# Half-batch tiles with two 24 KB runs of each of 64 lines, and one ring of three buffers for all tiles

## The chip, the cores and the metric

The kernel runs on one core of a Trainium2 chip. The metric is the device time of one execution in microseconds (us). Times of a kernel are given as the median of several executions; profiles show one execution in detail. The profile names the engines DVE (VectorE), ACT (ScalarE), POOL (GpSimd), SP (SyncE) and PE (TensorE, unused here); sixteen DMA engines move data between HBM and the on-chip memory of 128 partitions.

## The reference

The input x is float32 of shape (16, 64, 64, 64): batch b, channel c, height h, width w, 16.78 MB. The output holds all windows of 8 by 8 at a stride of 4, so 15 by 15 window positions (i, j):

```python
n_h = (h - window_size) // stride + 1
n_w = (w - window_size) // stride + 1
for i in range(n_h):
    for j in range(n_w):
        h_start = i * stride
        w_start = j * stride
        result[:, i, j] = x[:, :, h_start:h_start + window_size, w_start:w_start + window_size].copy()
```

The result has the shape (16, 15, 15, 64, 8, 8), 58.98 MB. Nothing is calculated; each input value is copied to up to four places. One window position of one image is 64 x 8 x 8 floats, 16 KB. For a fixed (b, i) the fifteen windows j lie one behind the other in memory; such a "line" is 15 x 16 KB = 240 KB, and there are 16 x 15 = 240 lines.

## The kernel before, in words

**The input on chip.** The tile L holds the whole input: partition p = 64 ch + 4 b + hq has the channels of half ch (32 of them) and the rows 16 hq to 16 hq + 15 of image b, in 4 KB per channel. The batch is also split in two halves y of 8 images (QP = 32 partitions for each ch and y). The loads are on three queues. ACT and SP first load the first FC = (8, 7) channels of each half into a staging area S, 64 partitions wide, which lies in the same memory as the output buffers (GG); DVE and ACT then copy it to its places in L (the loop over `moves`). SP and POOL load the other channels directly into L, for y = 0 first and then for y = 1 (the function `load`). All this comes before any output work in each engine's order.

**The output tiles.** A tile is a buffer in GG in which each partition holds one piece of one line, to be written as one row. DVE and ACT fill it by copies from L (with `stream_shuffle` on DVE where rows must move to the next partition or as another form of copy), and POOL writes it to HBM with an indirect DMA (`scatter`): an index per partition says which row of the output it is. The output is seen in two ways: `o_v` has rows of one window (CFREE = 4096 floats, 16 KB), `o_l` has rows, called runs here, of one and a half windows (LF = 6144 floats, 24 KB), NR = 10 to a line. Run k of a line begins with window 3k/2; `line(k)` lists its pieces: two half-windows of one channel half ch (places 0 and 2 of the row, from windows j and j + 1) and one half-window of the other (place 1). `windows(f, c, r, j, m)` is the view of L with m neighbouring windows, which overlap by half.

Four kinds of tiles are made:

- `part(y, j)`: a half-batch tile. Its 128 partitions hold the windows j and j + 1 of each of 64 lines (8 images, 4 hq, the line offsets s = 0 and 1 within a row block), as 16 KB rows. It needs only the half y of the input. Eight copies of 32 partitions x 2048 floats fill it, three on ACT and five on DVE. Its index is `idx_y`.
- `plain(k)`: run k of 128 lines (all 16 images, line offsets 0 and 1), 24 KB rows. Two copies on ACT, one copy and one shuffle on DVE. Its index is `idx`.
- `cross(k)`: run k of the lines with offsets 2 and 3; those with offset 3 take their lower half from the next row block, so a shuffle moves data by one partition. 112 of 128 rows are written. Its indices are `idx_lo` and `idx_hi` in turns.
- The last run of the lines with offsets 0 and 1 (loop at the end), written by two plain DMAs from SP, each of 64 rows.

**The order.** Three tiles part(0, 0), part(0, 2), part(0, 4) come first, as they need only the first half of the batch; then plain(4), part(1, 0), plain(5), part(1, 2), plain(6), part(1, 4); then plain(7), cross(0) to cross(4), plain(8), cross(5) to cross(9); then the last run. The half-batch tiles write windows 0 to 5, that is runs 0 to 3, of their lines.

**The buffers.** GG is 3 x 24 KB per partition. `tile_()` hands out the buffers: the first three tiles (EARLY) get three 16 KB places at its beginning, the fourth gets the third 24 KB buffer, and from there the tiles take the three 24 KB buffers in turn. A fill waits until the store that last read its memory has landed. The stores are declared free of each other, since each writes rows of its own. A DMA on POOL's queue also waits for the landing of the DMA eight before it, whose semaphore it uses.

**Queues.** POOL issues 16 loads and then the 21 scatters in the order of the tiles; they share one DMA queue (q0). SP issues its staging loads, 14 direct loads, and the two last stores (q1). ACT issues four staging loads (q10).

Of the kernel before, what the change touches and what calls it, by code (L numbers as in the profile page):

```python
# [10 lines left out]
def kernel(  # L11
# [8 lines left out]
    P = nc.NUM_PARTITIONS  # L20

    B, C, H, W = x.shape
    Bo, NH, NW, Co, WSo, WSo2 = out.shape
    WS = int(window_size)
    ST = int(stride)
# [4 lines left out]
    ALU = mybir.AluOpType  # L30
    CH = 2
# [4 lines left out]
    NWIN = NH * NW  # L36
    CFREE = C * WS * WS
    HP = P // CH
    YB = 8
    NY = B // YB  # L40
    QP = YB * HQ
# [10 lines left out]
    L = Lt[:, :, 0 : RB * W].rearrange("p c (r w) -> p c r w", r=RB)  # L52
# [12 lines left out]
    def itile(name):  # L65
        return ipool.tile([P, 1], i32, name=name)

    pi, tb, tq, tc_, te, tu, idx, idx_y, idx_lo, idx_hi = (
        itile(n) for n in ("pi", "tb", "tq", "tc", "te", "tu", "idx", "idx_y", "idx_lo", "idx_hi")
    )  # L70


    LF = 3 * CFREE // 2
    NR = NW * CFREE // LF
# [4 lines left out]
    def bits(d, shift, mask):  # L79
        nc.vector.tensor_scalar(out=d[:, :], in0=pi[:, :], scalar1=shift, scalar2=mask, op0=ALU.logical_shift_right, op1=ALU.bitwise_and)  # L80

    def mul(d, a, m):
        nc.vector.tensor_scalar(out=d[:, :], in0=a[:, :], scalar1=float(m), scalar2=None, op0=ALU.mult)

    def tt(d, a, b, op):
        nc.vector.tensor_tensor(out=d[:, :], in0=a[:, :], in1=b[:, :], op=op)  # L86
# [4 lines left out]
    def far(d, a, value):  # L91
        nc.vector.tensor_scalar(out=d[:, :], in0=a[:, :], scalar1=float(value), scalar2=FAR, op0=ALU.is_equal, op1=ALU.mult)
# [7 lines left out]
    tt(tu, tb, tc_, ALU.add)  # L100
    mul(idx, tu, NR)
    bits(tq, 5, 1)
    mul(tq, tq, 1 - YB * NWIN)
    mul(tu, tu, NW)
    tt(idx_y, tu, tq, ALU.add)
    far(tb, te, HP + HQ - 1)
    tt(idx_hi, idx, tb, ALU.add)
    far(te, te, HQ - 1)
# [5 lines left out]
    NG = 3  # L114
# [5 lines left out]
    GG = gpool.tile([P, NG * LF], f32)  # L120
# [3 lines left out]
    for q in range(HQ):  # L124
        for ch in range(CH):
            s = S[ch][QP + q : QP + q + (B - 1) * HQ + 1 : HQ]
# [14 lines left out]
    for n, (y, ch, c) in enumerate(moves):  # L141
        e = min(c + PC, FC[ch])
        f = slice(QP + y * QP, QP + (y + 1) * QP)
        d = slice(ch * HP + y * QP, ch * HP + (y + 1) * QP)
        copy = nc.vector.tensor_copy if n % 3 else nc.scalar.copy
        tc.keep_in_program_order(copy(out=L[d, c:e, :, :], in_=S[ch][f, c:e]))  # L146

    o_v = out.rearrange("b i j c r w -> (b i j) (c r w)")
    o_l = out.rearrange("b i j c r w -> (b i j c r w)").rearrange("(n f) -> n f", f=LF)
    nxt = [min(p + 1, 31) for p in range(32)]  # L150
    same = list(range(32))
    act, dve = nc.scalar.copy, nc.vector.tensor_copy

    def shf(out, in_, mask=same):
        nc.vector.stream_shuffle(out=out, in_=in_, mask=mask)  # L155

    def free(st):
        tc.declare_no_dep(st.ins, group="stores", reason="each store writes rows of its own")
        tc.add_to_no_dep_group("stores", st.ins)

    def scatter(g, ix, rows, first):
        f = rows.shape[1]
        st = nc.gpsimd.indirect_dma_start(  # L163
            out=rows,
            out_offset=bass.IndirectOffsetOnAxis(ap=ix[:, 0:1], axis=0),
            in_=g,
            in_offset=None,
            element_offset=first * f,
            bounds_check=rows.shape[0] - 1,
            oob_is_err=False,  # L170
        )
        free(st)

    EARLY = 3
    at = 0

    def tile_():
        nonlocal at
        at += 1
        if at <= EARLY:  # L180
            return GG[:, (at - 1) * CFREE : at * CFREE]
        n = (at - EARLY - 2) % NG
        return GG[:, n * LF : (n + 1) * LF]

    def halves(g, n):
        return g[:, 0 : n * CFREE // 2].rearrange("p (n c r w) -> p n c r w", n=n, c=CL, r=WS)

    def part(y, j):
        t = tile_()[:, 0:CFREE]
        g = halves(t, CH)  # L190
        order = [(d, ch) for ch in range(CH) for d in range(P // QP)]
        for n, (d, ch) in enumerate(order):
            s, dj = d // NY, d % NY
            cols = slice((j + dj) * ST, (j + dj) * ST + WS)
            f = (ch * NY + y) * QP
            tc.keep_in_program_order(
                (act if n % 3 == 0 else dve)(  # L197
                    out=g[d * QP : (d + 1) * QP, ch],
                    in_=L[f : f + QP, :, s * ST : s * ST + WS, cols],
                )  # L200
            )
        scatter(t, idx_y, o_v, j + y * YB * NWIN)

    def line(k):
        j, ch = 3 * k // CH, 3 * k % CH
        return (j, ch, slice(0, 3, 2), 2), (j + ch, 1 - ch, slice(1, 2), 1)

    def windows(f, c, r, j, m):  # L210
        v = L[f, c, r, j * ST : j * ST + WS]
        return bass.AP(tensor=v.tensor, offset=v.offset, ap=[v.ap[0], [ST, m], *v.ap[1:]])

    every = slice(0, CL)
    crossed = 0

    def plain(k):
        t = tile_()
        g = halves(t, 3)
        for half in range(CH):  # L220
            for j, ch, n, m in line(k):
                f = slice(ch * HP, (ch + 1) * HP)
                d = slice(half * HP, (half + 1) * HP)
                copy = (shf if m == 1 else act) if half == 0 else (dve if m == 2 else act)
                copy(out=g[d, n], in_=windows(f, every, slice(half * ST, half * ST + WS), j, m))  # L225
        scatter(t, idx, o_l, k)

    def cross(k):
        nonlocal crossed
        t = tile_()  # L230
        g = halves(t, 3)
        turn = 1 - crossed % 2
        crossed += 1
        lo, hi = slice(turn * HP, (turn + 1) * HP), slice((1 - turn) * HP, (2 - turn) * HP)
        s = NSLOT - 2
        for j, ch, n, m in line(k):
            f = slice(ch * HP, (ch + 1) * HP)
            act(out=g[lo, n], in_=windows(f, every, slice(s * ST, s * ST + WS), j, m))  # L238
            shf(out=g[hi, n, :, ST:WS], in_=windows(f, every, slice(0, ST), j, m), mask=nxt)
        for j, ch, n, m in line(k):  # L240
            f = slice(ch * HP, (ch + 1) * HP)
            dve(out=g[hi, n, :, 0:ST], in_=windows(f, every, slice((s + 1) * ST, RB), j, m))  # L242
        scatter(t, (idx_hi, idx_lo)[turn], o_l, s * NR + k)

    for n in range(EARLY):
        part(0, 2 * n)
    ready = 2 * EARLY * CFREE // LF
    for n in range(EARLY):
        plain(ready + n)
        part(1, 2 * n)  # L250
    rest = list(range(ready + EARLY, NR - 1))
    per = NR // len(rest)
    for n, k in enumerate(rest):
        plain(k)
        for m in range(n * per, (n + 1) * per):
            cross(m)


    ACT_C = 12
# [1 line left out]
    for s in range(2):  # L261
        t = tile_()
        g = halves(t, 3)
        for j, ch, n, m in line(NR - 1):
            for y in range(NY):
                d = slice(QP + y * QP, QP + (y + 1) * QP)
                f = slice(ch * HP + y * QP, ch * HP + (y + 1) * QP)
# [38 lines left out]
```

## Time and profile before

| | |
|---|---|
| Median of 3 runs | 184.75 us (184.5 to 184.81) |
| The profiled execution | 184.68 us, of which the span is 182.9 us |
| DVE busy | 138.7 us (76% of the span) |
| ACT busy | 137.5 us (75%) |
| POOL busy | 40.4 us (22%) |
| DMA | 75.80 MB in 9507 packets, mean 414 GB/s |
| HBM read, and written by the instructions' own account | 16.78 MB and 62.91 MB |

How to read it: "busy" is the time in which an engine executes instructions; issuing a DMA from SP or ACT does not count, but POOL's DMA instructions do, as POOL writes their descriptors. The span is cut into 40 slices, and each digit of a row is the busy share in tenths. "DMA" there is the mean over the sixteen DMA engines. Queue rows (q0, q1, q10) give packets, MB and the share of the sixteen engines' span. In the view of windows, a row gives for one stretch of time each engine's busy time with its number of instructions, the granted clock, the DMA share and the rate; packets are counted there from their start, so a share can be a little above 1. In the timeline and in the chain of waits a row begins with the start and the duration in us; in square brackets stands the idle time of the engine just before, and what ended it. In the rows of groups, after the count come the busy time, the mean ns of one, and the idle time before with what ended it. A row with "DMA out_dram<-GG,idx" as what ended a wait means that the engine waited for a store to land.

The bytes written by the instructions' own account count 16 rows for each crossing tile that are out of bounds and not written.

### The profile page before, as it was taken

The page shows a single profiled execution, that of the slowest core. Times are in us where ns is not written, and L with a number is a line of the kernel's source. Part 1 is how long each engine was busy: PE and PEld are TensorE (multiplying, and loading weights), DVE is VectorE, ACT ScalarE, POOL GpSimd, SP SyncE. Part 2 cuts the span into 40 slices and gives each one's busy share as a digit, 9 for nine tenths or more (in the row PEclk, how much of TensorE's full clock was granted, in tenths as well). Part 3 has the DMA queues.
Part 4 walks back from the last instruction along what each step waited for, and adds up shares of the span by engine and source line. Part 5 has one row for each costly group of instructions (what it writes and reads, how often), then busy time and mean ns, then how long its engine had stood idle before and what let it go on. Part 6 is the DMA issues. An engine that isn't in the chain of part 4 may idle for free.

```text
span 182.9 us, 453 instructions
## 1 busy us (share of the span) xinstructions
DVE 138.7 (76%) x141; ACT 137.5 (75%) x63; POOL 40.4 (22%) x42
## 2 busy tenths in 40 slices
DVE  3003997999998849979799888979769698894900
ACT  0003998999996869979899788969969697894900
POOL 7500754034340220231112202210220220240000
DMA  4999999999999999999999999999999999999995
GB/s 147 405 414 410 409 411 411 409 414 432 432 430 450 441 403 432 430 446 434 428 455 430 430 426 430 430 430 435 430 430 430 430 430 414 430 430 419 430 435 215
DMA packets 9507, 75.80 MB, mean 414 GB/s; under 512 B 2752, under 2 KB 2752, under 8 KB 6848
## 3 DMA queue, kind: packets, MB, share of 16 engines
q0 software_dynamic: 6736, 62.92, 81.3%
q1 hardware_dynamic: 2192, 10.75, 14.3%
q10 hardware_dynamic: 576, 2.10, 3.1%
q14 instruction: 3, 0.02, 0.0%
HBM read 16.78 MB, written 62.91 MB: 436 GB/s over the span
## 4 chain that ended last, share of the span: by engine, by line
DMA 75%; DVE 13%; POOL 3%; issue 2%; DVEq 1%; POOLq 0%; PEldq 0%
DMA out_dram<-GG,idx 28%; DMA out_dram<-GG,idx_lo 21%; DMA Lt<-in_x_dram 20%; DMA out_dram<-GG,idx_hi 6%; DVE GG L155 6%; POOL Lt L61 3%; DVE GG L242 2%; DVE GG L197 2%; DVE GG L269 2%; DVE GG L225 1%; DVEq L301 1%; POOL pi L77 0%; DVEq L155 0%; POOLq L163 0%; DVEq L269 0%
## 5 line engine op out<-in xcount | busy, mean ns | idle before, releaser
L238 ACT COPY GG<-Lt 64x4096 f32<-64x4096 f32 (+1 forms) x20 | 55.0, 2750 | 8.6 <-DMA out_dram<-GG,idx_lo 4.6
L155 DVE STREAM_SHUFFLE GG<-Lt 64x2048 f32<-64x2048 f32 (+1 forms) x25 | 49.2, 1969 | 0.6
L197 DVE COPY GG<-Lt 32x2048 f32<-32x2048 f32 x30 | 36.6, 1218 | 5.2 <-DMA out_dram<-GG,idx 3.6
L197 ACT COPY GG<-Lt 32x2048 f32<-32x2048 f32 x18 | 34.1, 1897 | 4.0 <-DMA out_dram<-GG,idx 2.8
L225 ACT COPY GG<-Lt 64x4096 f32<-64x4096 f32 (+1 forms) x10 | 27.5, 2750 | 3.8 <-DMA out_dram<-GG,idx_y 2.1
L146 DVE COPY Lt<-GG 32x2048 f32<-32x2048 f32 (+1 forms) x10 | 11.4, 1184 | 14.1 <-DMA GG<-in_x_dram 14.0
L242 DVE COPY GG<-Lt 64x2048 f32<-64x2048 f32 (+1 forms) x20 | 19.1, 955 | 0.5
L61 POOL DMA_DIRECT2D Lt<-in_x_dram x16 | 13.8, 871 | 15.9 <-DMA Lt<-in_x_dram 15.4
L163 POOL DMA_INDIRECT out_dram<-GG,idx_y x6 | 8.8, 1474 | 31.8 <-DVE GG L197 31.8
L146 ACT ACT_TABLE_LOAD x1 | 1.3, 1283 | 16.8 <-DMA GG<-in_x_dram 16.8
L163 POOL DMA_INDIRECT out_dram<-GG,idx_hi x5 | 6.2, 1248 | 28.7 <-DVE GG L242 17.9
L225 DVE COPY GG<-Lt 64x4096 f32<-64x4096 f32 x5 | 11.4, 2289 | 0.2
L269 ACT COPY GG<-Lt 32x1536 f32<-32x1536 f32 (+1 forms) x8 | 9.2, 1150 | 2.7 <-DMA out_dram<-GG,idx_lo 2.4
L269 DVE COPY GG<-Lt 32x2560 f32<-32x2560 f32 (+1 forms) x8 | 9.2, 1152 | 2.5 <-DMA out_dram<-GG,idx_lo 2.3
L163 POOL DMA_INDIRECT out_dram<-GG,idx x5 | 6.4, 1283 | 20.5 <-ACT GG L225 18.2
L163 POOL DMA_INDIRECT out_dram<-GG,idx_lo x5 | 4.8, 965 | 26.8 <-DVE GG L242 26.8
L146 ACT COPY Lt<-GG 32x2048 f32<-32x2048 f32 (+1 forms) x6 | 10.3, 1751 | 0.1
L155 DVE LOAD_MASK_SELECT GG<-Lt x25 | 0.2, 8 | 10.5 <-DMA out_dram<-GG,idx_lo 5.2
L80 DVE TENSOR_SCALAR tb<-pi 128x1 int32<-128x1 int32 x1 | 0.2, 154 | 1.0 <-POOL pi L77 1.0
L77 POOL IOTA pi<- 128x1 int32 x1 | 0.1, 124 | 0.4 <-PEq L301 0.4
L86 DVE CUSTOM_DVE_ANT_0 te<-te,tc 128x2 uint16<-128x2 uint16 x1 | 0.2, 160 | 0.0
L86 DVE CUSTOM_DVE_ANT_0 tb<-tb,tq 128x2 uint16<-128x2 uint16 x1 | 0.2, 159 | 0.0
(19 smaller groups left out, 2.6 us busy)
## 6 DMA issues: line engine op xcount, KB each, us to landing
Lt<-in_x_dram POOLq DMA_DIRECT2D x8, 800.0 KB, 16.1
out_dram<-GG SPq DMA_DIRECT2D x2, 1536.0 KB
Lt<-in_x_dram SPq DMA_DIRECT2D x6, 384.0 KB
GG<-in_x_dram ACTq DMA_DIRECT2D x4, 512.0 KB
Lt<-in_x_dram SPq DMA_DIRECT2D x6, 320.0 KB
GG<-in_x_dram SPq DMA_DIRECT2D x4, 448.0 KB
Lt<-in_x_dram SPq DMA_DIRECT2D x2, 704.0 KB
Lt<-in_x_dram POOLq DMA_DIRECT2D x8, 64.0 KB, 15.8
```

Of the source, the lines that this page charges most:

```text
L61: eng.dma_start(out=L[p0 : p0 + QP - HQ + 1 : HQ, c0:c1, :, :], in_=x_v[ch, y, q, :, c0:c1, :])
L80: nc.vector.tensor_scalar(out=d[:, :], in0=pi[:, :], scalar1=shift, scalar2=mask, op0=ALU.logical_shift_right, op1=ALU.bitwise_and)
L86: nc.vector.tensor_tensor(out=d[:, :], in0=a[:, :], in1=b[:, :], op=op)
L146: tc.keep_in_program_order(copy(out=L[d, c:e, :, :], in_=S[ch][f, c:e]))
L155: nc.vector.stream_shuffle(out=out, in_=in_, mask=mask)
L163: st = nc.gpsimd.indirect_dma_start(out=rows, out_offset=bass.IndirectOffsetOnAxis(ap=ix[:, 0:1], axis=0), in_=g, in_offset=None, element_ ...
L197: (act if n % 3 == 0 else dve)(out=g[d * QP : (d + 1) * QP, ch], in_=L[f : f + QP, :, s * ST : s * ST + WS, cols],)
L225: copy(out=g[d, n], in_=windows(f, every, slice(half * ST, half * ST + WS), j, m))
L238: act(out=g[lo, n], in_=windows(f, every, slice(s * ST, s * ST + WS), j, m))
L242: dve(out=g[hi, n, :, 0:ST], in_=windows(f, every, slice((s + 1) * ST, RB), j, m))
L269: copy(out=g[d, n, c0:c1], in_=windows(f, slice(c0, c1), slice(s * ST, s * ST + WS), j, m))
L301: with _tile.TileContext(nc) as tc:
```

## The change

`part(y, k)` now makes a tile with 24 KB rows: the runs k and k + 1 of each of the 64 lines of the half batch. Its pieces come from `line(k)` and `line(k + 1)`, so for each group of 32 partitions there is one copy of two windows (32 x 4096 floats) and one of one window (32 x 2048). The eight copies go by an order in which the pieces of channel half 0 come first; three of them go to ACT. The wide copies use the `windows` view, as plain tiles do.

Four such tiles, (0, 0), (0, 2), (1, 0) and (1, 2), replace the six of before; they write the runs 0 to 3 as before. The index `idx_y` is now made from `idx` with an offset in runs, one instruction less, and the view `o_v` is gone.

The order of the tiles is written out: part(0, 0), part(0, 2), plain(4), plain(5), part(1, 0), plain(6), part(1, 2), plain(7), cross(0) to cross(4), plain(8), cross(5) to cross(9), and the last run as before.

`tile_()` hands out the three 24 KB buffers in turn from the first tile on.

```diff
     bits(tq, 5, 1)
-    mul(tq, tq, 1 - YB * NWIN)
-    mul(tu, tu, NW)
-    tt(idx_y, tu, tq, ALU.add)
+    mul(tq, tq, 1 - YB * NH * NR)
+    tt(idx_y, idx, tq, ALU.add)
...
-    o_v = out.rearrange("b i j c r w -> (b i j) (c r w)")
...
-    EARLY = 3
     at = 0
 
     def tile_():
         nonlocal at
         at += 1
-        if at <= EARLY:
-            return GG[:, (at - 1) * CFREE : at * CFREE]
-        n = (at - EARLY - 2) % NG
+        n = (at - 1) % NG
         return GG[:, n * LF : (n + 1) * LF]
...
-    def part(y, j):
-        t = tile_()[:, 0:CFREE]
-        g = halves(t, CH)
-        order = [(d, ch) for ch in range(CH) for d in range(P // QP)]
-        for n, (d, ch) in enumerate(order):
-            s, dj = d // NY, d % NY
-            cols = slice((j + dj) * ST, (j + dj) * ST + WS)
-            f = (ch * NY + y) * QP
-            tc.keep_in_program_order(
-                (act if n % 3 == 0 else dve)(
-                    out=g[d * QP : (d + 1) * QP, ch],
-                    in_=L[f : f + QP, :, s * ST : s * ST + WS, cols],
-                )
-            )
-        scatter(t, idx_y, o_v, j + y * YB * NWIN)
...
+    def part(y, k):
+        t = tile_()
+        g = halves(t, 3)
+        order = [(d, *e) for c in range(CH) for d in range(P // QP) for e in line(k + d % NY) if e[1] == c]
+        for i, (d, j, ch, n, m) in enumerate(order):
+            s = d // NY
+            f = (ch * NY + y) * QP
+            tc.keep_in_program_order(
+                (act if i in (0, 6, 4 if k else 5) else dve)(
+                    out=g[d * QP : (d + 1) * QP, n],
+                    in_=windows(slice(f, f + QP), every, slice(s * ST, s * ST + WS), j, m),
+                )
+            )
+        scatter(t, idx_y, o_l, k + y * YB * NH * NR)
...
-    for n in range(EARLY):
-        part(0, 2 * n)
-    ready = 2 * EARLY * CFREE // LF
-    for n in range(EARLY):
-        plain(ready + n)
-        part(1, 2 * n)
-    rest = list(range(ready + EARLY, NR - 1))
-    per = NR // len(rest)
-    for n, k in enumerate(rest):
-        plain(k)
-        for m in range(n * per, (n + 1) * per):
-            cross(m)
+    for k in (0, 2):
+        part(0, k)
+    plain(4)
+    plain(5)
+    part(1, 0)
+    plain(6)
+    part(1, 2)
+    plain(7)
+    for k in range(NR // 2):
+        cross(k)
+    plain(8)
+    for k in range(NR // 2, NR):
+        cross(k)
```

## The prediction

> **What bounds the kernel now.** I read the page first: the span, the slices, the queues and the chain.
>
> ```profile
> span 182.9 us, 453 instructions
> DVE 138.7 (76%) x141; ACT 137.5 (75%) x63; POOL 40.4 (22%) x42
> DMA  4999999999999999999999999999999999999995
> GB/s 147 405 414 410 409 411 411 409 414 432 432 430 450 441 403 432 430 446 434 428 455 430 430 426 430 430 430 435 430 430 430 430 430 414 430 430 419 430 435 215
> DMA packets 9507, 75.80 MB, mean 414 GB/s; under 512 B 2752, under 2 KB 2752, under 8 KB 6848
> q0 software_dynamic: 6736, 62.92, 81.3%
> q1 hardware_dynamic: 2192, 10.75, 14.3%
> q10 hardware_dynamic: 576, 2.10, 3.1%
> DMA 75%; DVE 13%; POOL 3%; issue 2%; DVEq 1%; POOLq 0%; PEldq 0%
> ```
>
> The three queues together fill 81.3 + 14.3 + 3.1 = 98.7% of the sixteen DMA engines' span, and in every slice but the first and the last they are at nine tenths or more. The chain's 13% of DVE are no gap in the transfers: while that chain passes through DVE, stores issued earlier are still moving. The next view, the windows, shows it stage by stage.
>
> ```profile
> core 0: us, DVE busy (x) ACT busy (x) POOL busy (x), PEclk, DMA share, GB/s
> 3.00:43.00 40.00, 24.86 (x22) 25.22 (x15) 14.59 (x16) 1.00 1.03 408
> 45.00:91.00 46.00, 39.98 (x30) 40.56 (x18) 9.77 (x7) 1.00 1.00 431
> 91.00:175.00 84.00, 70.21 (x71) 69.71 (x30) 12.98 (x12) 1.00 1.01 432
> ```
>
> DMA share is 1.00 or more in the loads (3 to 43), in the stage that the change rewrites (45 to 91) and in the stage behind it. The rate with 16 KB rows among the stores (431 GB/s) and with 24 KB rows alone (432) is the same to 0.3%. So the span is bytes divided by rate, and an edit counts only if it changes the bytes, the rate, or makes the queue run dry.
>
> **The change part by part.** The bytes stay: six tiles of 128 rows of 16 KB are 12.6 MB, four of 128 rows of 24 KB too, and the other tiles keep their rows (lines 4 to 8, then the crossing ones, then the last). What one store occupies is read from the landings that released fills:
>
> ```profile
> 59.88 5.53 ACT L225 COPY GG<-Lt 64x4096 f32<-64x4096 f32 x2 [2.08 <-DMA out_dram<-GG,idx_y]
> 67.12 6.18 DVE L197 COPY GG<-Lt 32x2048 f32<-32x2048 f32 x5 [2.43 <-DMA out_dram<-GG,idx]
> 79.22 6.20 DVE L197 COPY GG<-Lt 32x2048 f32<-32x2048 f32 x5 [1.12 <-DMA out_dram<-GG,idx]
> 91.31 11.07 ACT L238 COPY GG<-Lt 64x4096 f32<-64x4096 f32 x4 [0.49 <-DMA out_dram<-GG,idx]
> ```
>
> The third store (16 KB rows) has landed at 59.88, the fourth (24 KB rows) at 67.12: 7.24 us. From there a store of each kind lands at 79.22 and another pair at 91.31, 12.1 us a pair, so 16 KB rows take 4.86. Six of those are 29.2 us, four of 7.24 are 29.0: minus 0.2. By the windows' rates the difference is nothing. I take minus 0.1, with minus 0.2 and 0 as its ends.
>
> The Trainium skill, page "DMA: Bandwidth & Descriptors", section "Anatomy of one DMA", gives such a store about 2.0 us of fixed time plus its bytes over 436 GB/s. Taken as a price for every store, two stores fewer would save 4 us; the landings 7.24 us apart leave no room for it, since 3.15 MB at the window's 432 GB/s are 7.28 us.
>
> The index edit drops one DVE instruction of 0.15 us:
>
> ```profile
> L83 DVE TENSOR_SCALAR tu<-tu 128x1 int32<-128x1 int32 x1 | 0.1, 148 | 0.0
> ```
>
> Its result feeds stores that wait for loads and fills long behind it, so it is worth nothing. Two store issues fewer on POOL, an engine busy for 22%, stand ahead of no work that could start sooner: nothing.
>
> What can cost something is whether each store is filled before the one ahead has left the queue. The fills are now longer, and the buffers are three of 24 KB from the start, where the first four stores had places of their own. Prices of copies:
>
> ```profile
> L197 DVE COPY GG<-Lt 32x2048 f32<-32x2048 f32 x30 | 36.6, 1218 | 5.2 <-DMA out_dram<-GG,idx 3.6 <-DMA Lt<-in_x_dram 1.0
> L155 DVE STREAM_SHUFFLE GG<-Lt 64x2048 f32<-64x2048 f32 x15 | 36.4, 2428 | 0.3
> L238 ACT COPY GG<-Lt 64x2048 f32<-64x2048 f32 x10 | 19.0, 1897 | 0.2
> L197 ACT COPY GG<-Lt 32x2048 f32<-32x2048 f32 x18 | 34.1, 1897 | 4.0 <-DMA out_dram<-GG,idx 2.8 <-DMA Lt<-in_x_dram 0.8
> L225 ACT COPY GG<-Lt 64x4096 f32<-64x4096 f32 x5 | 18.0, 3604 | 3.7 <-DMA out_dram<-GG,idx_y 2.1 <-DMA out_dram<-GG,idx_lo 1.5
> L225 DVE COPY GG<-Lt 64x4096 f32<-64x4096 f32 x5 | 11.4, 2289 | 0.2
> ```
>
> A half-batch tile becomes four copies of two windows (32x4096, a form not in this trace) and four of one. The nearest row for the two-window copy is the 64x4096 one, 2.29 on DVE and 3.60 on ACT; above it stand two 32x2048 copies, 2.44 and 3.79. I take the former: only the number of partitions differs, and ACT's 2048-element copy takes 1.897 us on 32 as on 64. With 0.02 between copies, a tile of run 0 gives DVE two wide and three narrow ones (8.3 us) and ACT two wide and one narrow (9.1); a tile of run 2 gives DVE three wide and two narrow (9.4), ACT one wide and two narrow (7.4). A plain tile stays at 5.5 us of ACT.
>
> Now the walk. In these rows the fills begin at 29.2, after the same loads, and the last load lands at 44.98:
>
> ```profile
> 29.23 5.74 ACT L197 COPY GG<-Lt 32x2048 f32<-32x2048 f32 x3 [0.76 <-DMA Lt<-in_x_dram]
> 29.64 15.35 DMA Lt<-in_x_dram
> 36.33 1.74 POOL L163 DMA_INDIRECT out_dram<-GG,idx_y  x1 [5.63 <-DVE GG L197]
> 48.62 2.39 POOL L163 DMA_INDIRECT out_dram<-GG,idx_y  x1 [4.36 <-DVE GG L197]
> ```
>
> The first store was issued at 36.33 and lay in the queue behind loads: three stores before 59.88 are 14.6 us, so the first began at 45.3 by its landing, just after the last load. The new first store is full at 29.2 + 9.1 = 38.4 and begins at the same 45.3, with seven microseconds of cover. From there the new landings are 7.24 apart: 52.5, 59.8, 67.0, 74.3, 81.5, 88.7, 96.0. The fills: the second tile ends when DVE has done both, 29.25 + 8.3 + 9.4 = 47.0. Plain 4 waits for nothing (its loads are there when ACT gets to it at 45.8) and ends at 51.8. Plain 5 needs the first store's buffer: 52.5 + 5.5 = 58.1. Half-batch tile (1, 0) needs the second's: 59.8 + 9.1 = 68.9. Plain 6 follows on ACT: 74.4. Tile (1, 2) needs the fourth's: 74.3 + 9.4 = 83.7. Plain 7 follows on DVE: 83.7 + 4.75 = 88.5. The first crossing tile needs the sixth's, 88.7, and takes 6.5, as from 91.31 to the issue at 97.83: 95.2.
>
> ```profile
> 97.83 0.97 POOL L163 DMA_INDIRECT out_dram<-GG,idx_lo  x1 [5.78 <-DVE GG L242]
> 103.44 5.52 ACT L238 COPY GG<-Lt 64x4096 f32<-64x4096 f32 x2 [1.05 <-DMA out_dram<-GG,idx]
> ```
>
> The spare time, from full until the store ahead lands, is thus 5.5 for the second store, then 8.0, 8.9, 5.4, 7.1, 5.0, 7.5 and 8.1. How much is needed is shown by the stores of before with the least:
>
> ```profile
> 74.08 0.96 POOL L163 DMA_INDIRECT out_dram<-GG,idx_y  x1 [7.43 <-DVE GG L197]
> 78.88 1.69 POOL L163 DMA_INDIRECT out_dram<-GG,idx  x1 [3.84 <-ACT GG L225]
> 86.19 0.96 POOL L163 DMA_INDIRECT out_dram<-GG,idx_y  x1 [5.63 <-DVE GG L197]
> 91.10 0.96 POOL L163 DMA_INDIRECT out_dram<-GG,idx  x1 [3.95 <-ACT GG L225]
> ```
>
> They were issued 5.1 (to 79.22), 5.2 (to 79.22 + 4.86), 5.1 (to 91.31) and 5.1 us (to 91.31 + 4.86) before the landing ahead, and the 45 to 91 window stayed at share 1.00. So some 5.1 us is enough at an issue of 0.96, and 5.2 at one of 1.69. The new 5.4 and 5.0 fall beside shuffles or idle DVE, the quick kind, and are worth nothing lost. The second store's 5.5 is the doubtful one. Behind the tile's last copy DVE starts plain 4's 2.29 us copy at once, as here:
>
> ```profile
> 47.88 2.29 DVE L225 COPY GG<-Lt 64x4096 f32<-64x4096 f32 x1
> 59.64 0.97 POOL L163 DMA_INDIRECT out_dram<-GG,idx_y  x1 [4.40 <-DVE GG L197]
> 59.94 2.43 DVE L155 STREAM_SHUFFLE GG<-Lt 64x2048 f32<-64x2048 f32 x1
> ```
>
> The issue at 48.62 lay under that copy and took 2.39, the one at 59.64 beside a shuffle 0.97. With 2.39 the second store has 5.5 - (2.39 - 1.69) = 4.8, against the 5.2 that were enough: between nothing and 0.4 us lost; with the dearer copy prices (five wide DVE copies, 0.15 each) up to 1.1. I take nothing, because 5.2 is only what sufficed, not a limit, and the sixteen engines do not run level:
>
> ```profile
> 179.00:180.00 1.00, 0.00 (x0) 0.00 (x0) 0.00 (x0) 1.00 0.91 393
> 180.00:181.00 1.00, 0.00 (x0) 0.00 (x0) 0.00 (x0) 1.00 0.52 221
> 181.00:182.00 1.00, 0.00 (x0) 0.00 (x0) 0.00 (x0) 1.00 0.01 0
> ```
>
> They finish over more than a microsecond, so the early ones can idle some tenths without moving the last.
>
> The Trainium skill, page "SBUF — State Buffer", section "SBUF: two separate sides", says that an fp32 copy on VectorE locks GpSimd out of a shared port, so that it can't write a store's descriptors until the copy ends. The 2.39 beside the copy and 0.97 beside the shuffle agree; it speaks for the late case below.
>
> Sum against the profiled run: 184.68 (182.9 of span, 1.8 around it) minus 0.1 is 184.6. The median shown is 184.75, 0.07 above the profiled run; minus 0.1 that is 184.65. I say 184.6.
>
> **The rivals.** First, the queue runs dry between the first and the second store, at 51 to 53 us. For it: 4.8 against 5.2, above, and that nothing else is left in the queue, as all loads have landed at 44.98. Against: the uneven engines, and that an issue made just ahead of the copy may get through first. Price 0.4 to 1.1, say 0.8, less the 0.1: 185.4. It decides from 0.5 us of dry queue.
>
> Second, each store carries a fixed price that the landings don't let me see. At the 0.96 us of a quick issue, two stores fewer save 1.9: 182.8. (By the 2.0 us of the Trainium skill's page "DMA: Bandwidth & Descriptors", section "Anatomy of one DMA", they would save 4.0.) Against: DMA share 1.00 at every stage, and pairs landing 12.1 apart for 5.24 MB, 433 GB/s.
>
> Third, the spare times behind the rewritten stage are larger than before (8.1 for the first crossing store, which had 5.6, from 97.83 to 103.44), and remove small gaps in the later stage. By the share of 1.01 from 91 to 175 there is none to remove beyond a tenth or two; if the rate there rose from 432 to 434, 84 us would lose 0.4: 184.2.
>
> **How the numbers follow.** A measurement of this kernel tells about 0.2%, 0.37 us, from no change: 184.38 to 185.12 is "the same". The forecast gets 0.60, the dry queue 0.22, the fixed price 0.06, the smaller gaps 0.12. Faster is 0.17, the last two with nearly all; slower 0.22; the same 0.61. The forecast's own range is 184.4 to 184.8. For eight in ten it reaches to 184.2 by the third rival and to 185.7 by the first with 1.1 us.
>
> **What would show it.** Right: DMA share 1.00 from 45 to 91, landings 7.2 apart from 52.5 on, ACT's first wait on a store near 52.5, POOL's second store issued near 47.0, and the first crossing fill starting near 88.7. Wrong: a window between 50 and 53 with a share well under 1 and every later landing moved by it (first rival); landings closer than 7.2 us (second); wide copies over 2.44 or 3.79 us, which would make the stores after 59.8 and 74.3 late as well.

## The result and the profile after

The changed kernel takes 185.77 us (median of 6 runs, 185.62 to 186.03), the kernel before 184.75 us in the same series (6 runs, 184.5 to 184.84). The ratio is 1.0059, with a 95% interval of 1.0049 to 1.007: slower by about 1.0 us. The profiled execution took 185.76 us, 1.08 us more than that of before, and its span grew by 1.1 us.

The page of the kernel after, with the lines that answer to the first fence of the prediction:

```profile
span 184.0 us, 427 instructions
DVE 137.1 (75%) x130; ACT 136.3 (74%) x57; POOL 39.9 (22%) x40
DMA  4999999999999999999999999999999999999994
GB/s 158 399 410 410 411 411 413 408 411 455 424 444 427 427 433 427 427 433 424 427 427 427 427 433 422 427 424 422 406 427 422 427 427 427 427 427 427 427 427 214
DMA packets 9219, 75.80 MB, mean 412 GB/s; under 512 B 2720, under 2 KB 2720, under 8 KB 6816
q0 software_dynamic: 6448, 62.92, 81.3%
q1 hardware_dynamic: 2192, 10.75, 14.3%
q10 hardware_dynamic: 576, 2.10, 3.1%
```

The three queue rows are the ones to read. They carry the same megabytes as before and fill the same 98.7% of the sixteen DMA engines, but of a span of 184.0 us in place of 182.9. An engine that had run dry would show a smaller share of the longer span. The share did not fall, so the transfers themselves took longer: 0.987 x 1.1 = 1.09 us, which is the whole loss. The row of rates says the same in another way: the value that recurs through the second half of the span is 427 GB/s, where it was 430.

The windows of the kernel after show the stages:

```profile
core 0: us, DVE busy (x) ACT busy (x) POOL busy (x), PEclk, DMA share, GB/s
3.00:43.00 40.00, 24.84 (x19) 25.33 (x12) 15.06 (x15) 1.00 1.03 408
45.00:91.00 46.00, 40.27 (x25) 41.21 (x16) 10.39 (x7) 1.00 1.00 429
91.00:175.00 84.00, 68.42 (x70) 67.80 (x30) 12.56 (x11) 1.00 1.00 425
```

The loads run as before (408). The rewritten stage has 429 for 431 GB/s, and most of the loss lies in the stage behind it, 425 for 432, whose code did not change. DMA share is 1.00 everywhere.

The timeline of the kernel after follows the prediction's walk almost to the tenth:

```profile
38.63 2.59 POOL L161 DMA_INDIRECT out_dram<-GG,idx_y  x1 [7.99 <-ACT GG L204]
47.01 2.29 DVE L221 COPY GG<-Lt 64x4096 f32<-64x4096 f32 x1
47.77 2.41 POOL L161 DMA_INDIRECT out_dram<-GG,idx_y  x1 [6.55 <-DVE GG L204]
49.34 2.41 DVE L153 STREAM_SHUFFLE GG<-Lt 64x2048 f32<-64x2048 f32 x1
52.42 5.52 ACT L221 COPY GG<-Lt 64x4096 f32<-64x4096 f32 x2 [1.07 <-DMA out_dram<-GG,idx_y]
...
58.21 0.96 POOL L161 DMA_INDIRECT out_dram<-GG,idx  x1 [4.72 <-ACT GG L221]
59.70 9.15 ACT L204 COPY GG<-Lt 32x4096 f32<-32x4096 f32 x3 [1.76 <-DMA out_dram<-GG,idx_y]
...
69.12 0.96 POOL L161 DMA_INDIRECT out_dram<-GG,idx_y  x1 [9.95 <-ACT GG L204]
...
74.20 9.37 DVE L204 COPY GG<-Lt 32x2048 f32<-32x2048 f32 x5 [1.35 <-DMA out_dram<-GG,idx]
...
89.09 5.52 ACT L234 COPY GG<-Lt 64x4096 f32<-64x4096 f32 x2 [1.68 <-DMA out_dram<-GG,idx]
...
103.58 5.53 ACT L234 COPY GG<-Lt 64x4096 f32<-64x4096 f32 x2 [1.68 <-DMA out_dram<-GG,idx]
```

The second tile is full at 47.01 (forecast 47.0), the first store has landed at 52.42 (52.5), the second at 59.70 (59.8), the fourth at 74.20 (74.3). Then the landings fall behind: 89.09 where 88.7 was forecast. The second store's issue starts at 47.77 and takes 2.41 us, under the copy that DVE began at 47.01.

Around that store no second of the queue stands empty, as the fine windows of the kernel after show:

```profile
50.00:51.00 1.00, 1.00 (x1) 1.00 (x1) 0.18 (x1) 1.00 0.97 418
51.00:52.00 1.00, 0.75 (x1) 0.35 (x1) 0.00 (x0) 1.00 1.04 442
52.00:53.00 1.00, 0.55 (x2) 0.58 (x1) 0.48 (x1) 1.00 1.08 467
```

The single DMA packets of the traces (one row of a store is one packet, recorded with its start, time and size) say how the rate fell. The record does not name a packet's engine, but strung together by their ends and starts the packets from 44 to 166 us make sixteen strands, one for each engine as it seems, in which one follows another within some 50 ns, before and after alike. What changes is the time of a packet. One of 24 KB that took 912 ns comes to take longer, mostly 914 to 946 ns, in one strand after another, and mostly stays so: in the kernel after, 21% of the 24 KB packets take 914 ns or more from 59 to 73 us, 57% from 73 to 91 and some 85% from 103 us on; before, it is under 8% up to 115 us. Mean time in ns of one 24 KB packet, by its start in us:

```
kernel              43-59  59-73  73-91  91-103 103-115 115-130 130-142 142-155 155-168
before              912.9  912.2  912.8  912.4  912.6   914.8   916.1   917.6   919.1
after               914.3  915.6  921.8  925.1  926.0   926.9   925.6   925.6   924.8
```

All packet times added up and divided by sixteen are 180.58 us before and 181.64 after: 1.06 of the 1.1 us. So the first question for the experiments was not which engine waits, but what makes the DMA engines slower from about 60 us on. In the expectations quoted below, "slow engines" or a "slow state" mean DMA engines with such longer packets.

### The profile page after: what moved, and what is told of

It reads as the page before. It is cut to its first block, busy times and chain, and to the rows that moved or that the text cites. A ratio compares the mean times of both kernels' runs of the same rounds, so it can differ in the third digit from the quotient of the medians.

```text
span 184.0 us, 427 instructions
## 1 busy us (share of the span) xinstructions
DVE 137.1 (75%) x130; ACT 136.3 (74%) x57; POOL 39.9 (22%) x40
## 4 chain that ended last, share of the span: by engine, by line
DMA 79%; DVE 8%; issue 5%; SPq 1%; DVEq 1%; POOLq 0%
DMA out_dram<-GG,idx_lo 22%; DMA Lt<-in_x_dram 16%; DMA out_dram<-GG,idx 16%; DMA out_dram<-GG,idx_y 12%; DMA out_dram<-GG,idx_hi 7%; DMA GG<-in_x_dram 6%; DVE GG L204 5%; DVE GG L267 2%; DVEq L299 1%; SPq L126 1%; DVE GG L153 1%; DVE GG L221 0%; SPq L61 0%; DVEq L153 0%; DVEq L221 0%
## 5 line engine op out<-in xcount | busy, mean ns | idle before, releaser
L204 DVE COPY GG<-Lt 32x2048 f32<-32x2048 f32 (+1 forms) x20 | 35.1, 1753 | 5.4 <-DMA out_dram<-GG,idx_y 2.5
L204 ACT COPY GG<-Lt 32x4096 f32<-32x4096 f32 (+1 forms) x12 | 33.0, 2749 | 2.8 <-DMA out_dram<-GG,idx_y 1.8
L161 POOL DMA_INDIRECT out_dram<-GG,idx_y x4 | 6.9, 1729 | 31.0 <-ACT GG L204 17.9
L161 POOL DMA_INDIRECT out_dram<-GG,idx_hi x5 | 6.8, 1360 | 30.6 <-DVE GG L238 18.8
L161 POOL DMA_INDIRECT out_dram<-GG,idx x5 | 7.0, 1406 | 20.8 <-ACT GG L221 14.7
```

Of the source, the lines that this page charges most:

```text
L161: st = nc.gpsimd.indirect_dma_start(out=rows, out_offset=bass.IndirectOffsetOnAxis(ap=ix[:, 0:1], axis=0), in_=g, in_offset=None, element_ ...
L204: (act if i in (0, 6, 4 if k else 5) else dve)(out=g[d * QP : (d + 1) * QP, n], in_=windows(slice(f, f + QP), every, slice(s * ST, s * ST ...
```

## The experiments

All comparisons are with the kernel before in the same series, whose medians lay between 184.62 and 184.75 us; intervals are 95%.

**Is it the ring, the row length, or the place of the buffers?** Three runs take the change apart. The first keeps the kernel before and its 16 KB tiles, and only lets all tiles take the ring of three from the first on:

```diff
-        if at <= EARLY:
-            return GG[:, (at - 1) * CFREE : at * CFREE]
-        n = (at - EARLY - 2) % NG
+        n = (at - 2) % NG
```

> The kernel before with its six 16 KB tiles, but all tiles in one ring of three buffers. If the buffers cost the time: about 185.8 us and 425 to 427 GB/s in the stage of crossing tiles (91 to 175 us). If the rows of the half-batch tiles cost it: 184.7 us as before and 432 GB/s there.

Measured: 186.19 us (186.06 to 186.2), ratio 1.0077 [1.0061, 1.0094]. The ring alone, without one longer row, costs at least as much as the whole change. In its timeline the fourth tile, which now waits for the first store's buffer, is late; its issue ends at 57.79, 2.0 us ahead of the landing of the third store (59.74 by this trace):

```profile
48.71 0.96 POOL L163 DMA_INDIRECT out_dram<-GG,idx_y  x1 [4.36 <-DVE GG L195]
55.63 2.16 POOL L163 DMA_INDIRECT out_dram<-GG,idx  x1 [5.95 <-ACT GG L223]
62.19 0.96 POOL L163 DMA_INDIRECT out_dram<-GG,idx_y  x1 [4.40 <-DVE GG L195]
```

The second kernel is that of before with its three tiles part(1, j) moved behind cross(1), cross(4) and cross(7), so that 24 KB rows run unbroken from 60 to beyond 90 us:

```diff
         plain(ready + n)
-        part(1, 2 * n)
...
+    plain(7)
+    late = {1: 0, 4: 2, 7: 4}
+    for m in range(NR):
+        if m == 5:
+            plain(8)
+        cross(m)
+        if m in late:
+            part(1, late[m])
```

> The kernel before with its three 16 KB tiles of the second half batch moved back among the crossing tiles (behind crossing tiles 1, 4 and 7). If an unbroken row of 24 KB packets slows the DMA engines and 16 KB rows in between keep them at their rate: packets of 24 KB stay nearer 912 ns than in the kernel before late in the run, 184.2 to 184.7 us. If the relative lags of the engines, as they happen to be, decide: no such order, 184.7 to 185.8. If buffers decide: 184.7.

Measured: 184.78 us, ratio 1.0004 [0.9994, 1.0014], with 24 KB packets of 912.1 ns from 59 to 73 us and 912.6 from 73 to 91. Long rows in a long line do not lower the rate. The third is the kernel after with the ring turned by one buffer, and nothing else:

```diff
-        n = (at - 1) % NG
+        n = at % NG
```

> The changed kernel with the ring begun one buffer later, so that every crossing tile lies in the buffer it had before the change. If the place of the buffers costs the time: 184.7 us. If not: 185.8 us, and packets of 915 to 925 ns from about 60 us on, as in the changed kernel.

Measured: 185.75 us, ratio 1.0054 [1.0037, 1.007]. The place of the buffers does not matter either.

**Do the loads ahead of the stores matter?** The kernel after with all eight of SP's direct loads of the first channel half cut in two, in place of six (the constant `SPLIT`, 6 before and 8 here):

> The changed kernel with the last two loads of SP cut in two like the others, so that the sixteen DMA engines leave the loads with other lags against each other. If the lags decide, the time moves by some tenths, between 184.6 and 186.5 us, and other engines slow at other times. If the row length decides: 185.8 us.

Measured: 186.19 us, ratio 1.0079 [1.0062, 1.0096], some 0.4 us more than the kernel after. The same slow packets appear, 915.2 ns at 59 to 73 us and 926.1 at 115 to 130. Its packet times add up to 181.68 us over sixteen, as in the kernel after (181.64), and its last packet of data ends within 0.1 us of that kernel's. So the extra 0.4 us lies behind the last transfer and is not a matter of the rate; what it is isn't known.

**One pair of instructions swapped.** What e1 and the kernel after share is one store early in the output that comes late for the one ahead of it. In the kernel after it is the second, and it is late partly because its issue lies under DVE's wide copy. This run puts DVE's shuffle of plain(4) ahead of that copy, and changes nothing else:

```diff
-                copy(out=g[d, n], in_=windows(f, every, slice(half * ST, half * ST + WS), j, m))
+                i = copy(out=g[d, n], in_=windows(f, every, slice(half * ST, half * ST + WS), j, m))
+                if k == 4 and copy in (shf, dve):
+                    tc.keep_in_program_order(i)
```

> The changed kernel with DVE's shuffle ahead of its wide copy in the first plain tile, so that POOL's issue of the second store at 47.8 us lies beside a shuffle (0.96 us) and not under a copy (2.41). If a late second store puts engines into the slow state: that issue about 1 us long, fewer slow engines before 70 us, 184.7 to 185.3 us. If the lags of the engines decide by themselves, or something else in the ring: 185.8 us and packets of 915 to 925 ns from 60 us on.

Measured: 184.79 us (10 runs, 184.6 to 185.01), ratio 1.0004 [0.9994, 1.0013]. The whole loss is gone. Its timeline, in the stretch that was changed:

```profile
47.00 2.43 DVE L153 STREAM_SHUFFLE GG<-Lt 64x2048 f32<-64x2048 f32 x1
47.75 1.00 POOL L161 DMA_INDIRECT out_dram<-GG,idx_y  x1 [6.55 <-DVE GG L204]
49.46 2.29 DVE L221 COPY GG<-Lt 64x4096 f32<-64x4096 f32 x1
```

The second store's issue starts at the same time (47.75 for 47.77), but beside the shuffle it takes 1.00 us in place of 2.41. The first store lands a tenth of a microsecond earlier, at 52.32, and the windows of this kernel show the rate restored for the whole run (its span is 182.9 us):

```profile
45.00:91.00 46.00, 40.77 (x26) 41.68 (x16) 8.98 (x7) 1.00 1.00 432
91.00:175.00 84.00, 67.86 (x69) 67.29 (x30) 12.15 (x11) 1.00 1.01 430
```

**Long rows in the late half only.** The kernel before with its first three 16 KB tiles in their own places, and the other half of the batch in two 24 KB tiles in the order of the kernel after (the new `part`, here called for y = 1 alone, with an index tile of its own):

> The kernel before with its first three 16 KB tiles and their early places kept, and only the second half batch in two 24 KB tiles, in the changed order. If the ring from the first tile on (a fourth tile that waits for the first store) starts the slow state: 184.6 to 184.8 us, 24 KB packets at 912 ns until 110 us or so. If the longer rows or fills of half-batch tiles start it: slow packets from 75 us on and 185.1 to 185.6 us.

Measured: 184.76 us, ratio 1.0002 [0.9992, 1.0012]. The two longer tiles (1, 0) and (1, 2) cost nothing, and gain nothing.

**Can a pause in POOL's queue give the rate back?** One theory was that the store ahead of the late one had eaten up a head start, and that a stretch of queue entries without bytes would restore it. The kernel after with four scatters behind plain(7) whose rows are all out of bounds, so that they write nothing:

```diff
     plain(7)
+    for _ in range(4):
+        scatter(Lt[:, 0, 0 : RB * W], idx_no, o_s, 0)
```

> The changed kernel with four scatters behind the last plain tile before the crossing ones whose rows are all out of bounds and write nothing, some 0.3 us without data for every DMA engine alike at about 102 us. If the slow state is an engine's lost head start, which a pause gives back: packets of 912 ns from 103 us on for 20 us or more, 185.3 to 185.8 us. If the engines' lags against each other make it, a pause common to all changes nothing: packets of 915 to 925 ns throughout and 186.1 us.

Measured: 186.49 us, ratio 1.009 [1.0073, 1.0107]: slower by another 0.7 us, with packets of 24 KB at 955.8 ns in the mean from 91 to 103 us and 926.8 from 130 to 142. That theory fell.

**How late is too late?** Starting from f1, the second store was made late by itself, with DVE's shuffle beside its issue and not the copy: POOL copies some columns of the tile into an unused tile ahead of the store. First 640 columns, then 384, later 1536:

```diff
+    late = ipool.tile([P, 640], mybir.dt.bfloat16, name="late")
...
+        if (y, k) == (0, 2):
+            nc.gpsimd.tensor_copy(out=late[:, :], in_=t[:, 0:640])
         scatter(t, idx_y, o_l, k + y * YB * NH * NR)
```

> The changed kernel with the shuffle first (184.8 us), and POOL made to copy 640 columns of the second tile to a place of its own before it issues that tile's store: the store is late by that copy's time, some 0.5 to 1 us, with no copy of DVE in its way. If lateness of the second store alone starts the slow state: slow engines before 70 us again and 185.3 to 185.9 us. If it needs DVE's copy over the issue: 184.8 us.

> As the one with 640 columns, with 384: late by 0.3 to 0.6 us. If lateness decides with a threshold, between 184.8 and the time of the other; if DVE's copy over the issue is needed, 184.8 us.

> As f1_shuffle_first, but POOL copies the first 1536 columns of the second tile into an unused tile ahead of the second store; that takes some 1.4 us, so the store is issued near 49.0 and its issue ends near 50.0, with no DVE copy over it. If the loss is set by when the issue ends (48.75 gave 184.79, 48.95 184.92, 49.06 185.03, 50.18 185.77), the time is 185.4 to 185.8. If the lock under DVE's copy has a share of its own in the changed kernel, it stays under 185.3.

The timeline of the last of them shows what is delayed, a store that is as quickly issued as in f1, only a microsecond later:

```profile
47.12 1.46 POOL L211 CAST late<-GG 128x1536 bf16<-128x1536 f32 x1 [5.88 <-DVE GG L205]
48.75 1.01 POOL L161 DMA_INDIRECT out_dram<-GG,idx_y  x1 [0.17 <-issue]
...
52.51 3.61 ACT L224 COPY GG<-Lt 64x4096 f32<-64x4096 f32 x1 [1.14 <-DMA out_dram<-GG,idx_y]
```

Together with f1 and the kernel after, ordered by the time from the end of the second store's issue to the landing of the first store, which is read where ACT's first wait on a store ends:

| kernel | issue ends | first store landed | between | median, us | ratio |
|---|---|---|---|---|---|
| g2, 384 columns | 48.95 | 52.55 | 3.6 | 184.92 | 1.0015 [1.0005, 1.0025] |
| f1, shuffle first | 48.75 | 52.32 | 3.6 | 184.79 | 1.0004 [0.9994, 1.0013] |
| g1, 640 columns | 49.06 | 52.41 | 3.4 | 185.03 | 1.0022 [1.0012, 1.0033] |
| h1, 1536 columns | 49.76 | 52.51 | 2.8 | 185.38 | 1.0042 [1.0029, 1.0056] |
| after | 50.18 | 52.42 | 2.2 | 185.77 | 1.0059 [1.0049, 1.007] |

The loss grows with the lateness of this one store. In g1 and h1 its issue took only 1.01 us, so a long issue is not needed for the loss; DVE's copy matters, as far as these runs show, by making the issue end later. The intervals of f1, g2 and g1 overlap from one to the next; those of h1 and the kernel after lie clear of f1's.

**One late store in the kernel before.** If that is the cause, one late store should spoil the kernel before as well, with its short rows and its separate places for the first stores. A first try copied the first 1536 columns of the fourth tile ahead of its store:

```diff
+        if k == 4:
+            nc.gpsimd.tensor_copy(out=late[:, :], in_=t[:, 0:1536])
         scatter(t, idx, o_l, k)
```

> The kernel before, with its buffers as they were, and POOL made to copy 1536 columns of the fourth tile before it issues that tile's store, so that this one store comes 1 to 2.5 us later. If a late store early on starts the slow state: 185.5 to 186.2 us, like the kernel before with the ring from the first tile on. If the ring does it in another way: 184.7 us.

Measured: 184.67 us, ratio 0.9997 [0.9987, 1.0008]. This was a miss of the edit, not of the theory. Those columns are filled early, so POOL made its copy while DVE was still at the tile:

```profile
51.05 1.48 POOL L228 CAST late<-GG 128x1536 bf16<-128x1536 f32 x1
53.46 1.84 POOL L163 DMA_INDIRECT out_dram<-GG,idx  x1 [0.93 <-DVE GG L155]
```

The store went out at 53.46, as in the kernel before (53.39), so nothing was late. It shows, though, that such a copy on POOL costs nothing by itself. The second try reads the columns that DVE's shuffle writes last:

```diff
+        if k == 4:
+            nc.gpsimd.tensor_copy(out=late[:, :], in_=t[:, 2048:3584])
+            nc.gpsimd.tensor_copy(out=late[:, 0:1024], in_=t[:, 2048:3072])
         scatter(t, idx, o_l, k)
```

> The kernel before with its 16 KB tiles, its buffers and its order of instructions; POOL copies 1536 and then 1024 of the columns that DVE's shuffle wrote last in the fourth tile into an unused tile ahead of the fourth store, so that it is issued near 55.9 in place of 53.39 and its issue ends near 57, without a wider tile or a ring of three. If one early store that comes as the queue runs out is enough to lower the rate behind it, 185.5 to 186.2 (the ring of three alone, whose fourth store was issued at 55.63, gave 186.19), with packets of 24 KB over 915 ns from about 60 us on. If the loss needs the longer tiles or the ring, it stays at 184.7.

Measured: 186.06 us (185.99 to 186.17), ratio 1.0077 [1.0063, 1.009]. POOL's rows in its timeline:

```profile
52.65 2.43 POOL L228 CAST late<-GG 128x1536 bf16<-128x1536 f32 x1 [1.75 <-DVE GG L155]
55.25 2.29 POOL L163 DMA_INDIRECT out_dram<-GG,idx  x1 [0.17 <-issue]
57.54 1.04 POOL L229 CAST late<-GG 128x1024 bf16<-128x1024 f32 x1
61.71 0.97 POOL L163 DMA_INDIRECT out_dram<-GG,idx_y  x1 [3.12 <-DVE GG L198]
```

The second copy was put behind the store, but the first and DVE's copies over the issue were enough: the issue ended at 57.54, 2.0 us ahead of the third store's landing (59.57 by this trace). The next store was issued at 61.71 in place of 59.64, still over 4 us ahead of the landing before it. From there on this kernel has the profile of the changed one, and its windows show the same rate behind:

```profile
45.00:91.00 46.00, 42.32 (x30) 40.48 (x18) 13.75 (x9) 1.00 1.01 430
91.00:175.00 84.00, 70.26 (x71) 69.73 (x30) 12.37 (x12) 1.00 1.00 425
```

Packet times for the runs that decide, in the same columns as above, and the sum of all packet times over sixteen beside the span:

```
kernel              59-73  73-91  103-115 130-142   sum/16   span
before              912.2  912.8  912.6   916.1     180.58   182.9
f1 shuffle first    912.2  912.6  913.3   917.9     180.59   182.9
h1 1536 columns     912.4  915.6  923.1   925.0     181.26   183.6
after               915.6  921.8  926.0   925.6     181.64   184.0
e1 ring only        918.5  925.0  928.3   927.0     181.76   184.2
h2 before, 4th late 917.9  924.2  927.7   927.0     181.88   184.1
```

Span less sum is 2.2 to 2.5 us in all six. So nearly all that these kernels differ by is packet time.

## Why the prediction was wrong

**What held.** The bound was right: the DMA queue is full in every stage, and so the loss, too, is a loss of the DMA engines. The walk of the landings held to 0.1 us up to the one at 74.2. The wide copies on 32 partitions cost what the prediction took from the 64-partition rows, as the groups of the kernel after, split by form, show:

```profile
L204 DVE COPY GG<-Lt 32x4096 f32<-32x4096 f32 x10 | 22.9, 2288 | 0.3
L204 ACT COPY GG<-Lt 32x4096 f32<-32x4096 f32 x6 | 21.6, 3604 | 2.6 <-DMA out_dram<-GG,idx_y 1.8 <-DMA Lt<-in_x_dram 0.8
```

The doubtful store was the right one, and its issue took the 2.41 us that were feared (2.39). The shuffle in its place (f1) brought it to 1.00, which agrees with what the prediction cited of the Trainium skill, page "SBUF — State Buffer", section "SBUF: two separate sides".

**The step that failed** is the term of the second store, "I take nothing, because 5.2 is only what sufficed, not a limit". Two things were wrong in it.

First, its footing. The spare time of 5.5 us was counted from the moment the tile is full (47.0), the need of 5.1 or 5.2 us from the start of an issue. POOL starts the issue 0.76 us after the tile is full (47.01 to 47.77 above). The start is also the wrong end to count from: f1 starts its issue 4.6 us ahead of the landing, less than the 5.1 of the prediction's rows, and loses nothing that can be told. Counted from the end of the issue, the least of before is the store at 78.88 + 1.69 = 80.57, 3.5 us ahead of the landing at 79.22 + 4.86; the second store of the kernel after has 2.2. On that footing it was short by 1.3 us, not by 0.4, and for this store the table above shows the loss beginning at 3.4 (g1). Of the stores with more spare time the prediction weighed no issue, and that of plain(6) took 3.18 us (74.67 to 77.85), under DVE's copies; it still ended some 3.5 us ahead of the landing before it, in f1 too, which loses nothing.

Second, what a shortage does. The argument that "the sixteen engines do not run level" hides a gap of some tenths supposes that a late store leaves a gap, and that the rate behind it stays at 432 GB/s. Neither was so. There was no gap in the kernel after (e1, with a store still a little later, has one of 0.12 us in one strand of packets, at 58.3 us), and most packets of the rest of the run took longer. The loss is spread: against f1, whose landings stand at the same places, the kernel after is 0.1 us late at the first landing (52.42 for 52.32), 0.5 at 103.58 (103.08 in f1), and 1.1 at the end.

**The rivals.** The first one had the place, the store and nearly the price (0.4 to 1.1 us, against 1.0 measured), but not the mechanism: the window that it asked for, "between 50 and 53 with a share well under 1", does not exist. That its price fits is no proof of it; h1 and h2 show the loss as longer packets. The second rival, a fixed price per store, is out: f1 has two stores fewer than the kernel before and the same time. The third, smaller gaps behind the rewritten stage, is out by the same run. The term of minus 0.1 for the changed rows is not to be seen in f1 (1.0004 [0.9994, 1.0013]) and is too small to be told.

**The range** of the forecast, 184.4 to 184.8, missed by 1.0 us, as its term for the second store was nothing. The wider one ended at 185.7, the dearer end of the first rival less 0.1, and 185.77 lies just above. That it came so near is luck: the price was that of a gap, and there was none.

**What stays open** is what happens inside a DMA engine. The runs show that one early store whose issue ends 2.8 us or less ahead of the landing before it lowers the rate, that most packets behind it stay slower, and that lateness sets how early they appear (from about 60 us in the kernel after, about 73 in h1). They don't show why, and they give no one limit for all stores. In e2 two stores among the crossing tiles were nearly as late:

```profile
95.84 0.96 POOL L163 DMA_INDIRECT out_dram<-GG,idx_y  x1 [6.81 <-DVE GG L197]
102.40 0.96 POOL L163 DMA_INDIRECT out_dram<-GG,idx_lo  x1 [5.60 <-DVE GG L242]
108.15 0.96 POOL L163 DMA_INDIRECT out_dram<-GG,idx_hi  x1 [4.79 <-issue]
113.88 2.19 POOL L163 DMA_INDIRECT out_dram<-GG,idx_lo  x1 [4.76 <-DVE GG L242]
```

By this trace the store issued at 95.84 landed at 106.3 and the one issued at 108.15 at 119.0, so the second and the fourth of these issues ended 3.0 us ahead (3.1 by the measure of the table, which reads a landing some 0.1 us later). Yet e2 loses nothing: its 24 KB packets take 912.9 ns from 103 to 115 us and 913.1 from 115 to 130. Whether the place in the run or the last tenths of a microsecond decide was not tried. The kernel before also comes to 919.1 ns late in its run (155 to 168 us); what brings it there was not tried, and lateness need not be the only way. None of the kernels beats the kernel before; those that avoid the late store equal it.

## What to carry to other kernels

When a queue is full everywhere, ask of each transfer not only whether the next one is queued before the queue is empty, but how long before, counted from the end of its issue; for a store early in this kernel some 3.6 us cost next to nothing and 2.8 us cost 0.4%, while later in the run 3.1 us cost nothing that can be seen (e2). If it is short, look first at what the neighbouring engine does during the issue: swapping a copy and a shuffle on DVE took 1.4 us off an issue and gave back the whole 1.0 us of the run. And when the share of busy time stays at 1.00 while the span grows, compare the time of single transfers of one size, since a full queue can still be a slower one.

## What was not expected of the hardware

A DMA engine can be busy without a break and yet slower: 24 KB packets of 912 ns turn into packets of mostly 914 to 946 ns, in one strand of packets after another, and mostly stay so (some 85% of them from 103 us on in the kernel after). Over the run that is 1.06 us.

The 24 KB, 16 KB and 4 KB packets take 912, 611 and 159 ns when undisturbed, so 8 KB more cost 301 ns from 16 to 24 KB, and about 9 ns of each packet are left that do not grow with its size. This is why 16 KB and 24 KB rows came out at nearly the same rate.

POOL's copy of 1536 columns took 1.46 us beside a shuffle (h1) and 2.43 us beside DVE's copies (h2), and in h2 the five copies of DVE in the same stretch took 8.39 us in place of 6.22 in the kernel before:

```profile
52.54 8.39 DVE L198 COPY GG<-Lt 32x2048 f32<-32x2048 f32 x5
```

POOL and DVE hold each other up in both directions there.
